# Two transformer blocks on one core: modulation steps placed one by one, more first products ahead, and the end of the first MLP loop rearranged

## The chip, the cores and the metric

The kernel runs on one core of a Trainium2 chip, as one program from inputs in device memory to the output in device memory. The metric is the device time of one execution in microseconds (us). Five engines work side by side and each runs its own instructions in a fixed order: PE (matrix products), DVE (VectorE), ACT (ScalarE), POOL (GpSimd) and SP (here only a queue that starts transfers). An instruction that waits holds up everything behind it on its engine. Engines meet through semaphores; a transfer (DMA) is issued by the queue of an engine and then moves by itself.

## The reference, cut to what matters

Two blocks follow one another on x of 1024 tokens by 1024 columns, all in float32. The work touched by the change is the MLP of the first block, that of the second, and the modulation of the second.

```python
def first_block(x, ...):
    ...
    x = x + jnp.einsum("bsd,de->bse", merged, w_out[l])
    h = rmsnorm(x, g_mlp[l])
    hid = jnp.square(jax.nn.relu(jnp.einsum("bsd,df->bsf", h, w_mlp_in[l])))     # 1024 x 1024 x 4096
    x = x + jnp.einsum("bsf,fd->bsd", hid, w_mlp_out[l])                         # 1024 x 4096 x 1024
    return rmsnorm(x, g_final)

def second_block(x, c, ...):
    mod = jax.nn.silu(c) @ w_ada[l] + b_ada[l]       # one row of 1024 times 1024 x 6144
    sh1, sc1, gt1, sh2, sc2, gt2 = jnp.split(mod, 6, axis=-1)
    h = _modulate(_rmsnorm(x, g_mix[l]), sh1, sc1)
    x = x + gt1[:, None, :] * _mixer(h, ...)
    h = _modulate(_rmsnorm(x, g_ffn[l]), sh2, sc2)
    a = jnp.square(jax.nn.relu(jnp.einsum('bsd,df->bsf', h, w_ff1[l])))
    x = x + gt2[:, None, :] * jnp.einsum('bsf,fd->bsd', a, w_ff2[l])
    return _rmsnorm(x, g_final)
```

## The kernel before, in words

In the time of the profiled execution the kernel has these stretches: attention of the first block up to about 700 us, the merge and the output projection to 880, the MLP of the first block (MLP1) to about 1640, the mixer of the second block to 2037, and the MLP of the second block (MLP2) to 2713. Both MLPs are the one function `mlp`, called twice.

The activations are held transposed (features on the 128 partitions, tokens along the row), and all matrices are split in two fp32r parts: hi is a cast, lo is what is left. A product is then three passes of the matrix engine, hi·hi, lo·hi and hi·lo. `product` (L1231 ff.) makes one 128 x 512 block over four feature chunks, so 4 x 3 = 12 matmuls of 128 x 512 (L1233 to L1235). `parts_of` splits a weight tile: the cast "wh" on ACT (L1227) and the rest "wl" on DVE, or on POOL where it is told so (L1228).

Each GEMM is done by a scheme of seven products for eight. In the first GEMM, 16 steps m run in a loop. The seven products of a step are P1 and P2 (both in `first_two`: P1 is copied to s1, P2 plus s1 becomes q11, L1264 to L1277), P5, and products with the operands t2, B22, t3 and t4. P1 and P2 need only the first half of the activations, HT[0]; the others need HT[1], t2, t3 and t4, all made from the second half. Those operands are made by `make_t` and, for its second part, `rest` (L1104 ff.), a chain of about 45 DVE instructions that begins when the row statistics of the second half have gone through POOL (L127) and a transpose on PE (L1035). `rest` holds four of the six product banks in PSUM for its intermediates. Before the loop, `first_two` is called for m = 0 to 3; from m = 3 on the loop calls it for m + 1. `sums` (L1279, its four additions at L1284 to L1287) makes the combined weight tiles on POOL. The results of a step, q11, q12, q21, q22, t1 to t4 and so on, are stored in device memory by `save` (L1258), on ACT's queue, with t1 to t4 put off to the next step by `later`.

In the second GEMM, four blocks `ch` of hidden columns run over seven products for each of four output tiles e. `second` (L1358 ff.) loads one stored operand of 1 MB and splits it: the cast at L1370, the difference at L1371, alternately on DVE and POOL. Weights w2 come in quarters of 1 MB by SP's queue (L1407), and the sums of quarters s_, a21 and a11 are made on POOL (L1432, L1450, L1451, L1454). The results of the products are added by DVE: `upd` (L1377) into the residual, which lies in the tiles that the loop used before, and is loaded from "ml_x" by 16 transfers (L1356); `gather` (L1388); L1460.

The modulation (`ada`, L1182 to L1209) is a row times a matrix, done on DVE: 12 groups of 8 steps. A step multiplies a 128 x 512 weight tile "adaw" (256 KB, loaded by SP's queue) by one number per partition and adds it to "ada" (L1199 the first, L1201 the others). After 8 steps PE transposes the group in four blocks (L1207), and DVE reduces and adds the bias (L1208, L1209). `tick` advances this generator by one step; the loop of MLP1 ticks four times per m, in two pairs.

Within an engine the instructions stand in an order that a scheduler of the builder has fixed from a model of durations; in program order the ticks are where the code calls them, but the scheduler moves an instruction whose inputs are there early. `order` rows, shown with the change, are that fixed order.

## Time and profile before

| | |
|---|---|
| median of 3 runs | 2725.16 us (2717.71 to 2726.5) |
| the profiled execution | 2721.95 us |
| its span in the trace | 2720.2 us |
| mean granted clock of PE | 0.972 of full speed |
| busy in the span: PE, DVE, ACT, POOL | 93%, 69%, 44%, 36% |

The profiled execution is 1.75 us longer than its span. Times in the views are microseconds from the start of the span. A clock of 1.00 is the upper level of PE's clock, 2.4 GHz; 0.50 would be the lower, 1.2 GHz, and a stretch with a value between has had both. A row on a wait says which engine and line waited for which other engine and line. Matmuls are pipelined, so the duration of one is longer than the spacing of two.

### The profile page before, as it was taken

To read this page: it belongs to the slowest core of one execution; us is meant where nothing else is said; L and a number is where in the kernel's file an instruction comes from. 1 tells how busy PE (TensorE), PEld (TensorE's weight loads), DVE (VectorE), ACT (ScalarE), POOL (GpSimd) and SP (SyncE) were. 2 spreads that over 40 slices of the span, in tenths; PEclk is the share of its full clock that TensorE was granted. 3 is DMA by queue.
4 is the path that set the end of the run, shared out by engine and by line. 5 is a ranking of instruction groups with operands and counts; after the bars stand their busy time and mean duration, and the time that the engine had idled before them with its cause. 6 is when DMAs were issued, how large, how long until landed. Compare 5 with 4: busy or idle time off the path is not lost. (4 is left out here: it accounts for less than half of the span.)

```text
span 2720.2 us, 34915 instructions
## 1 busy us (share of the span) xinstructions
PE 2528.9 (93%) x12560; PEld 2107.4 (77%) x12560; DVE 1882.7 (69%) x3206; ACT 1197.9 (44%) x2218; POOL 988.1 (36%) x717
## 2 busy tenths in 40 slices
PE   7999999899999678888899979999997999989997
PEld 6899987788878566667688856888786788768886
DVE  7685878834455866676778896755658565578898
ACT  6575765335334433334433333323335554543433
POOL 3011123421002533333755661211334443476554
PEclk9999999999999889999999989999998999999999
DMA  3121022321155266666644301422343444753431
GB/s 114 53 61 40 25 79 90 89 61 41 63 183 179 78 203 200 202 204 230 220 170 155 109 24 51 156 63 70 120 152 97 160 150 159 250 204 134 170 109 62
DMA packets 275712, 338.57 MB, mean 124 GB/s; under 512 B 14268, under 2 KB 185044, under 8 KB 268372
## 3 DMA queue, kind: packets, MB, share of 16 engines
q1 hardware_dynamic: 234820, 253.65, 29.2%
q10 hardware_dynamic: 40720, 82.70, 8.3%
q8 instruction: 99, 1.62, 0.2%
q14 instruction: 73, 0.60, 0.1%
HBM read 250.25 MB, written 86.05 MB: 124 GB/s over the span
## 5 line engine op out<-in xcount | busy, mean ns | idle before, releaser
L1233 PE MATMUL mm<-h_hi,wh 128*128 128x512 f32 (+1 forms) x1136 | 455.5, 401 | 33.3 <-ACT wh L1227 17.2
L1235 PE MATMUL mm<-h_hi,wl 128*128 128x512 f32 (+1 forms) x1136 | 452.1, 398 | 10.5 <-DVE wl L1228 10.5
L1234 PE MATMUL mm<-h_lo,wh 128*128 128x512 f32 (+1 forms) x816 | 322.2, 395 | 0.0
L1233 PEld LDWEIGHTS mm<-h_hi,wh 128*128 128x128 f32 x1136 | 221.4, 195 | 82.2 <-ACT wh L1227 20.6
L1235 PEld LDWEIGHTS mm<-h_hi,wl 128*128 128x128 f32 x1136 | 220.7, 194 | 63.4 <-DVE wl L1228 18.2
L1227 ACT CAST wh<-q 128x1024 fp32r<-128x1024 f32 x116 | 121.7, 1052 | 331.7 <-PE mm L1234 297.7
L1234 PE MATMUL mm<-h_hi,wh 128*128 128x512 f32 (+1 forms) x624 | 244.8, 392 | 13.2 <-POOL h_hi L1371 13.2
L1228 DVE TENSOR_TENSOR wl<-q,wh 128x1024 fp32r<-128x1024 f32 x116 | 162.9, 1405 | 32.9 <-ACT wh L1227 31.3
L1234 PEld LDWEIGHTS mm<-h_lo,wh 128*128 128x128 f32 x816 | 158.3, 194 | 31.6
L1371 POOL TENSOR_TENSOR h_hi<-h_lo,h_hi 128x512 fp32r<-128x512 f32 x76 | 128.6, 1712 | 113.1 <-ACT h_hi L1370 107.9
L133 ACT CAST wh<-wr 128x1024 fp32r<-128x1024 f32 (+5 forms) x107 | 97.2, 911 | 149.7 <-PE mm L418 43.5
L1233 PE MATMUL mm<-q,wh 128*128 128x512 f32 x384 | 151.3, 394 | 10.4 <-DVE q L1119 10.4
L1235 PE MATMUL mm<-q,wl 128*128 128x512 f32 x384 | 150.2, 392 | 8.0 <-DVE wl L1228 8.0
L1234 PE MATMUL mm<-q,wh 128*128 128x512 f32 x384 | 150.9, 393 | 0.0
L1234 PEld LDWEIGHTS mm<-h_hi,wh 128*128 128x128 f32 x624 | 120.5, 193 | 37.9 <-POOL h_hi L1371 14.4
L1284 POOL TENSOR_TENSOR sa<-wr 128x512 f32<-128x512 f32 x32 | 41.7, 1303 | 264.8 <-DMA wr<-in_w_ff_dram 60.5
L134 POOL TENSOR_TENSOR wl<-wr,wh 128x1024 fp32r<-128x1024 f32 (+5 forms) x40 | 78.1, 1958 | 160.7 <-ACT wh L133 159.2
L1615 PE MATMUL mm<-h_hi,wh 128*128 128x512 f32 x320 | 132.0, 412 | 0.8 <-DVE kn L1648 0.8
L1617 PE MATMUL mm<-h_hi,wl 128*128 128x512 f32 x320 | 126.7, 396 | 0.0
L1371 DVE TENSOR_TENSOR h_hi<-h_lo,h_hi 128x512 fp32r<-128x512 f32 x76 | 120.4, 1605 | 8.3 <-ACT h_hi L1370 8.3
L1616 PE MATMUL mm<-h_lo,wh 128*128 128x512 f32 x320 | 125.5, 392 | 0.0
L1233 PE MATMUL mm<-h_lo,wh 128*128 128x512 f32 (+1 forms) x304 | 115.4, 380 | 0.6 <-ACT wh L1227 0.6
(589 smaller groups left out, 7006.9 us busy)
## 6 DMA issues: line engine op xcount, KB each, us to landing
h_lo<-ml_t SPq DMA_DIRECT2D x32, 1024.0 KB
adaw<-in_w_ada_dram SPq DMA_DIRECT2D x96, 256.0 KB
h_lo<-ml_q SPq DMA_DIRECT2D x24, 1024.0 KB
wr<-in_w_in_dram SPq DMA_DIRECT2D x42, 512.0 KB
wr<-in_w_out_dram SPq DMA_DIRECT2D x32, 512.0 KB
ml_t<-h_lo ACTq DMA_DIRECT2D x64, 256.0 KB
q<-in_w_mlp_out_dram SPq DMA_DIRECT2D x16, 1024.0 KB
ml_t<-x ACTq DMA_DIRECT2D x64, 256.0 KB
```

Source lines behind the costliest of these rows:

```text
L133: A.copy(hi, r)
L134: (eng or V).tensor_tensor(lo, r, raw(hi), op=OP.subtract)
L1227: A.copy(hi, r)
L1228: (eng or V).tensor_tensor(lo, r, raw(hi), op=OP.subtract)
L1233: mm(a, wt[0][:, k], b[0][:, k, sl], start=(k == 0), stop=False)
L1234: mm(a, wt[0][:, k], b[1][:, k, sl], start=False, stop=False)
L1235: mm(a, wt[1][:, k], b[0][:, k, sl], start=False, stop=(k == 3))
L1284: G.tensor_tensor(sa[:, 0:4], e2[:, 0:4], e2[:, 4:8], op=OP.add)
L1371: (G if c % 2 else V).tensor_tensor(lo[:, c], r[:, c], raw(hi[:, c]), op=OP.subtract)
L1615: mm(a, hi[:, k, :], r_hi, start=(k == 0), stop=False)
L1616: mm(a, hi[:, k, :], r_lo, start=False, stop=False)
L1617: mm(a, lo[:, k, :], r_hi, start=False, stop=(k == DC - 1))
```

## The change

Four things are changed, and line numbers of the kernel after are larger by some 20 (matmuls L1255 to L1257, wh L1249, wl L1250).

1. The modulation steps (now L1180 and L1182). `tick` takes the result of an eviction, and the step is queued on DVE behind that eviction (`tc.issue_after`), one step at a time: four per m in MLP1's loop, the rest, 40 of 96 steps, in the first three blocks of the second GEMM. The tiles are loaded two steps ahead. The transpose of the bias and the silu of c move from the begin of MLP1 into the output projection.
2. `first_two` runs for m = 4, 5 and 6 first, with s1 and q11 stored in device memory ("away", ACT's queue), and then for 0 to 3: 14 products ahead of the first P5, in place of 8. The loop then loads s1 and q11 of 4, 5, 6 back by SP's queue in steps 3, 4 and 5.
3. The last step's put-off stores and those of q22 and q21, six in all, are issued on POOL's queue.
4. The residual comes back in four transfers of 1 MB, in place of 16 of 256 KB: `x_back(0)` behind the load of t1, `x_back(1)` behind that of t2; the additions of block 0 into the second half of the residual, `upd(1, e)`, move from the q12 products to the t2 products.

```diff
+        load(0)
+        load(1)
+        for g in range(12):
+            acc = modp([P, 512], tag="ada", bufs=1)
+            for k in range(DC):
+                w = ld.pop(0)
...
+                load(g * DC + k + 2)
+                yield
...
+    def tick1(after):
+        with tc.issue_after(after.ins):
+            next(ada_, None)
...
         def save(n, m, t_):
-            nc.scalar.dma_start(d[n][:, m, :], t_)
+            (nc.gpsimd if later and m == NM - 1 else nc.scalar).dma_start(d[n][:, m, :], t_)
...
+            if away:
+                nc.scalar.dma_start(d["away"][:, m - 4, 0, :], s1)
+                nc.scalar.dma_start(d["away"][:, m - 4, 1, :], q11)
...
-        first_two(0, w_of(wp, 0, "wr", 2))
+        first_of(4, away=True)
         begin[0]()
-        first_two(1, w_of(wp, 2, "wr", 2), begin[1])
-        first_two(2, w_of(wp, 4, "wr", 2), eng=G)
+        first_of(5, away=True)
+        begin[1]()
+        first_of(6, eng=G, away=True)
+        first_of(0)
         rest_t.pop()()
         begin[2]()
-        first_two(3, w_of(wp, 6, "wr", 2), eng=G)
+        first_of(1)
+        first_of(2)
+        first_of(3)
...
-                if m >= 3:
+                if m >= 6:
                     first_two(m + 1, e1s[m + 1])
+                elif m >= 3:
+                    for i, t_ in enumerate((s1s, q11s)):
+                        nc.sync.dma_start(t_[(m + 1) % 4], d["away"][:, m - 3, i, :])
...
-            V.tensor_tensor(q12, p5, u2, op=OP.add)
-            for _ in range(2):
-                tick()
+            tick(V.tensor_tensor(q12, p5, u2, op=OP.add))
             ub = parts_of(e1s.pop(m))
             a = mm_bank()
             product(a, half(ub, 1), B22)
-            V.tensor_tensor(q12, a, q12, op=OP.add)
+            tick(V.tensor_tensor(q12, a, q12, op=OP.add))
...
+        def x_back(hf):
+            for e0 in (0, 4):
+                nc.sync.dma_start(xt[hf][:, e0:e0 + 4, :], d["x"][:, e0:e0 + 4, halves(hf)])
...
             b = second("t2", ch)
+            if not ch:
+                x_back(1)
             for e, wt in blocks(a11):
                 a = mm_bank()
                 product(a, wt, b)
-                V.tensor_tensor(U[e], a, U[e], op=OP.add)
+                if not ch:
+                    upd(1, e, U[e])
+                r = V.tensor_tensor(U[e], a, U[e], op=OP.add)
+                if e != 1:
+                    tick(r)
```

First place: DVE at the head of MLP1, at the end of the chain of `rest`. The q_ names are t3 and t4; wl tiles with wr_ are weights of `first_two`, sa_ and we_ those of the loop. Before:

```order
L1119 TENSOR_TENSOR q_9108<-mm_9261,q_9107 128x512
L1143 TENSOR_TENSOR mm_9262<-t_1892_9189,mm_9262 128x512
L1274 TENSOR_TENSOR h_hi_8328<-mm_9340,h_hi_8328 128x512
L1228 TENSOR_TENSOR wl_9366<-sa_9360,wh_9365 128x1024
```

And now:

```order
L1120 TENSOR_TENSOR q_9118<-mm_9313,q_9117 128x512
L1144 TENSOR_TENSOR mm_9314<-t_1897_9219,mm_9314 128x512
L1295 TENSOR_TENSOR h_hi_8333<-mm_9392,h_hi_8333 128x512
L1250 TENSOR_TENSOR wl_9411<-wr_9408,wh_9410 128x1024
L1120 TENSOR_TENSOR q_9118<-mm_9314,q_9117 128x512
L1250 TENSOR_TENSOR wl_9447<-wr_9444,wh_9446 128x1024
L1295 TENSOR_TENSOR h_hi_8333<-mm_9428,h_hi_8333 128x512
```

Behind the chain there now stand wl_9411 and wl_9447, the weights of `first_of(2)` and `first_of(3)`, four products that are meant to run ahead of the loop. Before, no wl of `first_two` stood behind it: those of m = 0 and 1 came earlier on DVE, and those of 2 and 3 were made by POOL.

Second place: DVE in the loop, one step m. Before:

```order
L1209 TENSOR_TENSOR mod_9086<-mod_9086,bada_9087 128x4
L1228 TENSOR_TENSOR wl_9978<-we_9762,wh_9977 128x1024
L1201 SCALAR_TENSOR_TENSOR ada_10357<-adaw_10455,silu_9404,ada_10357 128x512
L1339 TENSOR_TENSOR h_lo_8329<-mm_9895,h_hi_8328 128x512
L1340 TENSOR_TENSOR h_lo_8329<-mm_9895,h_lo_8329 128x512
L1201 SCALAR_TENSOR_TENSOR ada_10357<-adaw_10458,silu_9404,ada_10357 128x512
L1201 SCALAR_TENSOR_TENSOR ada_10357<-adaw_10512,silu_9404,ada_10357 128x512
L1201 SCALAR_TENSOR_TENSOR ada_10357<-adaw_10515,silu_9404,ada_10357 128x512
L1201 SCALAR_TENSOR_TENSOR ada_10357<-adaw_10612,silu_9404,ada_10357 128x512
L1274 TENSOR_TENSOR h_hi_8328<-mm_9939,h_hi_8328 128x512
L1228 TENSOR_TENSOR wl_10000<-wr_9849,wh_9999 128x512
```

And now:

```order
L1345 TENSOR_TENSOR h_lo_8334<-mm_9617,h_hi_8333 128x512
L1182 SCALAR_TENSOR_TENSOR ada_9527<-adaw_9583,silu_8844,ada_9527 128x512
L1250 TENSOR_TENSOR wl_9737<-sa_9685,wh_9736 128x1024
L1349 TENSOR_TENSOR h_lo_8334<-mm_9658,h_lo_8334 128x512
L1182 SCALAR_TENSOR_TENSOR ada_9527<-adaw_9603,silu_8844,ada_9527 128x512
L1359 TENSOR_TENSOR h_lo_8334<-mm_9690,h_hi_8333 128x512
L1360 TENSOR_TENSOR h_lo_8334<-mm_9617,h_lo_8334 128x512
L1182 SCALAR_TENSOR_TENSOR ada_9527<-adaw_9652,silu_8844,ada_9527 128x512
L1250 TENSOR_TENSOR wl_9775<-we_9630,wh_9774 128x1024
L1365 TENSOR_TENSOR h_lo_8334<-mm_9711,h_lo_8334 128x512
L1182 SCALAR_TENSOR_TENSOR ada_9527<-adaw_9673,silu_8844,ada_9527 128x512
```

Four or more steps in a row, each waiting for its own tile, have become single steps with an eviction ahead of each.

Third place: POOL between the two GEMMs of MLP1. h_hi_ and h_lo_ with L1371 (now L1401) are operands of the second GEMM, q_ at L1432 to L1451 (now L1462 to L1484) the sums of weight quarters. Before:

```order
L1371 TENSOR_TENSOR h_hi_11911<-h_lo_11811,h_hi_11911 128x512
L1320 TENSOR_TENSOR h_lo_8329<-h_hi_8328,h_lo_8329 128x512
L1343 TENSOR_TENSOR h_lo_8329<-h_lo_8329 128x512
L1432 TENSOR_TENSOR q_11818<-q_11814,q_11816 128x1024 x2
L1450 TENSOR_TENSOR q_11814<-q_11812,q_11814 128x1024 x2
L1451 TENSOR_TENSOR q_11812<-q_11818,q_11812 128x1024 x2
L1371 TENSOR_TENSOR h_hi_11911<-h_lo_11811,h_hi_11911 128x512
```

And now:

```order
L1401 TENSOR_TENSOR h_hi_11836<-h_lo_11815,h_hi_11836 128x512
L1280 DMA ml_q_1745_8348<-h_lo_8334 128x512
L1401 TENSOR_TENSOR h_lo_11997<-h_lo_11815,h_lo_11997 128x512
L1280 DMA ml_q_1743_8346<-h_lo_8334 128x512
L1280 DMA ml_t_1744_8347<-h_lo_8334 128x512
L1373 TENSOR_TENSOR h_lo_8334<-h_lo_8334 128x512
L1280 DMA ml_t_1742_8345<-h_lo_8334 128x512
L1280 DMA ml_t_1746_8349<-h_lo_8334 128x512
L1462 TENSOR_TENSOR q_11822<-q_11818,q_11820 128x1024 x2
L1483 TENSOR_TENSOR q_11818<-q_11816,q_11818 128x1024 x2
L1484 TENSOR_TENSOR q_11816<-q_11822,q_11816 128x1024 x2
```

The second half of the operand h_hi (before: h_hi_11911, now: h_hi_11836) has moved from behind the six sums to ahead of them, and DMA issues stand between.

## Rows read from the trace of the kernel before

**Rows 1.** The profile's head and its busy times by engine.

```profile
span 2720.2 us, 34915 instructions
PE 2528.9 (93%) x12560; PEld 2107.4 (77%) x12560; DVE 1882.7 (69%) x3206; ACT 1197.9 (44%) x2218; POOL 988.1 (36%) x717
```

**Rows 2.** The view by stretches: stretch, its length, busy time (count) of PE, of PE's weight loads, of DVE, ACT and POOL, granted clock, share of DMA, GB/s. In order: head and loop of MLP1, the passage to its second GEMM, a part of that GEMM, and, inside it, a part with nothing but full-speed products; then head, loop and passage of MLP2.

```profile
880.00:983.00 103.00, 67.22 (x268) 52.96 (x267) 81.31 (x102) 39.70 (x64) 48.16 (x32) 0.82 0.41 133
983.00:1293.00 310.00, 272.08 (x1136) 214.59 (x1134) 213.55 (x278) 124.94 (x188) 110.74 (x78) 0.96 0.62 206
1293.00:1345.00 52.00, 42.93 (x167) 33.82 (x168) 36.70 (x38) 21.94 (x34) 38.53 (x18) 0.88 0.73 260
1360.00:1564.00 204.00, 204.00 (x901) 168.92 (x901) 172.70 (x174) 80.12 (x115) 121.73 (x61) 1.00 0.41 145
1428.00:1496.00 68.00, 68.00 (x301) 56.31 (x301) 59.88 (x59) 27.17 (x40) 39.42 (x20) 1.00 0.43 155
2037.70:2121.00 83.30, 64.08 (x261) 50.34 (x260) 61.23 (x79) 43.32 (x70) 42.45 (x30) 0.88 0.33 100
2121.00:2370.70 249.70, 247.92 (x1093) 204.72 (x1092) 141.53 (x174) 129.67 (x189) 108.80 (x79) 1.00 0.53 176
2370.70:2423.40 52.70, 42.91 (x168) 33.76 (x169) 37.47 (x38) 21.99 (x35) 38.72 (x18) 0.90 0.73 264
```

**Rows 3.** PE's waits at the head of MLP1 (880 to 983 us): engine, line that waited, what it waited for, us in total, times, longest.

```profile
PE tp L1207 <- DVE ada L1201: 13.8, 2, 12.2
PE tp L1035 <- POOL st_r L127: 10.2, 1, 10.2
PE mm L1233 <- ACT h_hi L1269: 6.1, 1, 6.1
PE mm L1233 <- DVE q L1119: 5.7, 1, 5.7
```

**Rows 4.** The same view in the loop of MLP1 (983 to 1293 us).

```profile
PE mm L1235 <- DVE wl L1228: 14.2, 16, 1.9
PE tp L1207 <- DVE ada L1201: 12.6, 7, 2.1
PE mm L1233 <- ACT wh L1227: 10.9, 4, 6.0
```

**Rows 5.** DVE's longest wait in that loop, same columns.

```profile
DVE ada L1201 <- DMA adaw<-in_w_ada_dram: 57.0, 32, 4.1
```

**Rows 6.** DVE's groups of instructions in that loop: line, operation, output and inputs, shape, count, busy time and mean duration in ns, then the idle time before them.

```profile
L1201 DVE SCALAR_TENSOR_TENSOR ada<-adaw,silu,ada 128x512 f32<-128x512 f32 x70 | 55.5, 793 | 57.6 <-DMA adaw<-in_w_ada_dram 57.0
L1209 DVE TENSOR_TENSOR mod<-mod,bada 128x4 f32<-128x4 f32 x11 | 12.7, 1155 | 0.0
L1208 DVE TENSOR_REDUCE mod<-tp 128x4 f32<-128x512 f32 x11 | 7.4, 676 | 0.0
```

**Rows 7.** DVE's groups in the second GEMM (1360 to 1564 us), same columns.

```profile
L1228 DVE TENSOR_TENSOR wl<-q,wh 128x1024 fp32r<-128x1024 f32 x38 | 51.0, 1341 | 3.7 <-ACT wh L1227 3.6
L1371 DVE TENSOR_TENSOR h_hi<-h_lo,h_hi 128x512 fp32r<-128x512 f32 x26 | 42.6, 1664 | 0.0
L1377 DVE TENSOR_TENSOR h_lo<-mm,h_lo 128x512 f32<-128x512 f32 x36 | 24.2, 681 | 15.6 <-PE mm L1235 15.6
```

**Rows 8.** The timeline of DVE at the head of MLP1: start, us, line, operation, output and inputs, count. The first row is the first instruction behind the transpose L1035, the second the last of the chain of `rest`; the others are a wl and modulation steps right behind it.

```profile
900.19 1.41 DVE L1109 SCALAR_TENSOR_TENSOR h_lo<-h_lo,cols,tp 128x512 f32<-128x512 f32 x2 [6.83 <-PE tp L1035]
...
931.61 0.68 DVE L1119 TENSOR_TENSOR q<-mm,q 128x512 fp32r<-128x512 f32 x1
...
934.11 1.78 DVE L1228 TENSOR_TENSOR wl<-wr,wh 128x512 fp32r<-128x512 f32 x1
935.81 3.47 DVE L1201 SCALAR_TENSOR_TENSOR ada<-adaw,silu,ada 128x512 f32<-128x512 f32 x2
```

**Rows 9.** The timeline of POOL at the head of MLP1, up to the statistics (L127).

```profile
889.11 1.71 POOL L1284 TENSOR_TENSOR sa<-wr 128x512 f32<-128x512 f32 x1
...
897.96 1.02 POOL L127 TENSOR_TENSOR st_r<-st_r,mhalf 128x4 f32<-128x4 f32 x1
```

**Rows 10.** PE's waits between the GEMMs of MLP1 (1293 to 1345 us).

```profile
PE mm L1234 <- POOL h_hi L1371: 7.4, 1, 7.4
PE mm L1233 <- ACT wh L1227: 6.0, 1, 6.0
```

**Rows 11.** The timeline of POOL there.

```profile
1300.43 5.20 POOL L1432 TENSOR_TENSOR q<-q,q 128x1024 f32<-128x1024 f32 x2 [0.40 <-DMA q<-in_w_mlp_out_dram]
...
1311.29 6.07 POOL L1451 TENSOR_TENSOR q<-q,q 128x1024 f32<-128x1024 f32 x2
1317.32 1.26 POOL L1371 TENSOR_TENSOR h_hi<-h_lo,h_hi 128x512 fp32r<-128x512 f32 x1
```

**Rows 12.** The timeline of ACT there: the cast of the first weight quarter, what it waited for, and a store's issue by ACT's queue.

```profile
1275.33 0.33 ACTq L1258 DMA_DIRECT2D ml_t<-h_lo  x1
...
1291.90 1.04 ACT L1227 CAST wh<-q 128x1024 fp32r<-128x1024 f32 x1 [7.49 <-DMA q<-in_w_mlp_out_dram]
```

**Rows 13.** The waits of SP's queue from 1262 to 1320 us (the loads of the residual, L1356).

```profile
SPq L1356 <- DVE h_lo L1339: 10.1, 2, 8.8
```

**Rows 14.** PE's waits at the head of MLP2 (2037.7 to 2121 us).

```profile
PE mm L1233 <- ACT x L1269: 8.2, 1, 8.2
PE mm L1233 <- DVE q L1119: 4.7, 1, 4.7
```

**Rows 15.** PE's waits between the GEMMs of MLP2 (2370.7 to 2423.4 us).

```profile
PE mm L1234 <- POOL h_hi L1371: 5.8, 1, 5.8
PE mm L1233 <- ACT wh L1227: 3.6, 2, 1.8
```

More of the change, by code (lines that the diff above doesn't have):

```diff
@@ L1145, in make_t, with ada, load @@
         rest_t.append(rest)
+    mod = cst([P, 48], tag="mod")
+    bada = cst([P, 48], tag="bada")
+    def ada(modp):
+        badr = modp([48, P], tag="badr")
+        nc.scalar.dma_start(badr, b_ada_2[0].rearrange("(k p) -> k p", p=P))
+        yield
+        pt = tp_bank()
+        T.transpose(pt[:, :48], badr, ident[:48, :48])
+        V.tensor_copy(bada, pt[:, :48])
+        r0, _ = ROWS["c_2"]
+        s_ = modp([P, 64], tag="silu")[:, :DC]
+        A.activation(s_, cols[:, r0:r0 + 8], AF.Tanh, scale=0.5)
+        V.scalar_tensor_tensor(s_, s_, 1.0, cols[:, r0:r0 + 8], op0=OP.add, op1=OP.mult)
+        V.tensor_scalar(s_, s_, 0.5, None, op0=OP.mult)
+        yield
+        ld = []
+        def load(i):
+            if i < 12 * DC:
+                w = modp([P, 512], tag="adaw", bufs=2)
+                nc.sync.dma_start(w, w_ada_2[0, (i % DC) * P:(i % DC + 1) * P, halves(i // DC)])
+                ld.append(w)
+        load(0)
[4 more added lines that the diff above has]
+                w = ld.pop(0)
+                if k == 0:
+                    V.tensor_scalar(acc, w, s_[:, 0:1], None, op0=OP.mult)
+                else:
+                    V.scalar_tensor_tensor(acc, w, s_[:, k:k + 1], acc, op0=OP.mult, op1=OP.add)
+                load(g * DC + k + 2)
+                yield
+            yield
+            m4 = mod[:, g * 4:(g + 1) * 4]
+            pt = tp_bank()
+            for j in range(4):
+                T.transpose(pt[:, j * P:(j + 1) * P], acc[:, j * P:(j + 1) * P], ident)
+            V.tensor_reduce(m4, pt.rearrange("p (j q) -> p j q", j=4), axis=AX.X, op=OP.add)
+            V.tensor_tensor(m4, m4, bada[:, g * 4:(g + 1) * 4], op=OP.add)
+    modp = Pool("modp", side="right")
+    ada_ = ada(modp)
+    def tick1(after):
+        with tc.issue_after(after.ins):
+            next(ada_, None)
     xT = [hB([P, DC, 512], tag=n) for n in ("h_hi", "h_lo")]
@@ L1162, in x_cols @@
         A.copy(xT[hf][:, e, :], pt)
+        if e == 2:
+            next(ada_)
     mlp_d = mlp_dram(drm)
@@ L1257, in save, with first_two @@
         def save(n, m, t_):
[L1258 removed]
+            (nc.gpsimd if later and m == NM - 1 else nc.scalar).dma_start(d[n][:, m, :], t_)
         def save_later():
             while later:
[L1262 to L1264 removed]
+                save(*later[0])
+                later.pop(0)
+        def first_two(m, e1, eng=None, away=False):
             s1, q11 = s1s[m % 4], q11s[m % 4]
@@ L1327, in mlp @@
             V.tensor_tensor(u3, a, u2, op=OP.add)
-            V.tensor_tensor(q22, p5, u3, op=OP.add)
+            tick(V.tensor_tensor(q22, p5, u3, op=OP.add))
             relu2(q22)
             save("q22", m, q22)
-            for _ in range(2):
-                tick()
             a = mm_bank()
             product(a, u4, TQ["t4"])
-            V.tensor_tensor(u3, a, u3, op=OP.add)
+            tick(V.tensor_tensor(u3, a, u3, op=OP.add))
             A.activation(u3, u3, AF.Relu)
@@ L1433, in mlp @@
             b = second("q12", ch)
+            if not ch:
+                bt = second("t1", ch)
+                x_back(0)
             for e, wt in blocks(a11):
@@ L1534, in post_mlp1 @@
         if hf == 0:
-            for _ in ada_["it"]:
+            for _ in ada_:
                 pass
```

75 lines of the change are left out of this document (16 added, 59 removed).

## The prediction

> **What bounds the kernel now.** I read the busy times first: PE is busy for 2528.9 of the 2720.2 us, DVE for 69% [rows 1]. So time can only come from PE's gaps and from the time in which PE runs below its full clock. For where these lie I read the view by stretches. Between 1428 and 1496 us PE does 301 matmuls of 128 x 512 in 68.00 us at a clock of 1.00: 0.226 us each, 2.71 us for a product of 12 [rows 2]. What a stretch loses is its length less its matmuls times 0.226, and this counts gaps and slow clock together:
> - head of MLP1: 103.0 - 268 x 0.226 = 42 us, clock 0.82;
> - loop of MLP1: 310.0 - 1136 x 0.226 = 53 us, clock 0.96;
> - passage to its second GEMM: 52.0 - 167 x 0.226 = 14 us, clock 0.88;
> - the second GEMM, 1360 to 1564: nothing, 901 x 0.226 = 204;
> - head of MLP2: 83.3 - 261 x 0.226 = 24 us; its loop: 249.7 - 1093 x 0.226 = 3 us; its passage: 52.7 - 168 x 0.226 = 15 us [all rows 2].
>
> Together 151 us, of which the change touches all. The two loops are the same code, and only that of MLP1 has modulation steps: 53 us against 3. Last I read, for each of these stretches, which wait of PE it is (rows named below).
>
> **The change part by part.**
>
> *Modulation in the loop.* PE waits 14.2 us in 16 pieces for wl, 12.6 us for the last step of a group and 10.9 us for wh, 37.7 us together [rows 4]; the other 15 of the 53 are the slower clock behind each gap. The first two come from DVE's order: steps stand four or more in a row, and each can wait for its tile. DVE stood 57.0 us in 32 such waits, 1.8 us each, the longest 4.1 [rows 5]; behind the waiting step stand the wl and the evictions that PE needs. Afterwards one step stands behind each of four evictions per m, and its tile was asked for two steps earlier. DVE's load allows it: in MLP2's loop it works 141.5 of 249.7 us [rows 2], about 10.8 us in the 19.0 of a step m; four modulation steps of 0.793 and half a group's end of (0.676 + 1.155) [rows 6] add 4.1. What stays: two of the seven group ends in this loop have their transposes directly behind the product of the eviction before the last step, and wh is untouched by this part. I put the loop at 12 us (from 53), between 5 (a little over MLP2's 3) and 25 (both wh and group ends as before: 10.9 + 12.6): -41.
>
> *More P1 and P2 ahead.* At the head PE waits 13.8 us for modulation steps, 10.2 for the statistics on POOL, 6.1 for an ACT result of `first_two` and 5.7 for the chain of `rest` [rows 3]. The first goes: no transpose of a group stands there now. Of the second, POOL's sums, 889.1 to 897.9 us before L127 [rows 9], go behind it, some 8 us, and what is late next is the reduce on DVE. The third is hidden by more products. But the cover for the chain is thinner than 14 products. The chain takes from 900.2 to 932.3 us, 32 us, of DVE with hardly a gap [rows 8]. Behind the transpose L1035 PE has six products, 6 x 2.71 = 16 us; the weights of the next four, wl_9411 and wl_9447, stand behind the chain in DVE's order. So PE stands for about 32 - 16 = 16 us, where the slower clock then adds 3 to 4. Head from 42 to 20 us, -22. Bounds: 12 if only the chain's first part is waited for, 28 if the loop's wl, which follow those two, come late too. In MLP2 the same order holds; its 24 us, 8.2 of them for ACT and 4.7 for the chain [rows 14], become 20: -4, between -10 and +2.
>
> The stores and loads of s1 and q11 for 4 to 6 are 12 more transfers of 256 KB. They lie beside the head and the loop, where the DMA engines have shares of 0.41 and 0.62 [rows 2]; I cost them at nothing. Without that cover, 1.5 MB each way at the loop's 206 GB/s is 15 us.
>
> *The passage.* In MLP1 PE waits 7.4 us for the second half of an operand that POOL makes only behind six sums of weights, from 1300.4 to 1317.3 us, and 6.0 us for the first weight quarter's cast [rows 10, 11]. That cast stood 7.5 us for its transfer [rows 12], since SP's queue was held by the residual's loads, which waited 10.1 us for tiles still in use [rows 13]. Now the operand is ahead of the sums and the loads behind the quarters, so both waits go. What is late next: the wl of a11 stands in DVE's order ahead of the evictions of the t1 products, and needs the same sums. They start behind six DMA issues, which this trace shows nowhere on POOL. Bounds for one: 0.33 us, what an issue takes on ACT's queue [rows 12], and 3.04, half of the two L1451 in 6.07 [rows 11], the longest POOL instruction here. 2 to 18 us in all; I take the lower, since the row is a DMA issue as well. `x_back(1)` waits for these stores, and DVE's additions into the second half wait for it; before them PE has about eight products, 22 us. The passage goes from 14 to 9. In MLP2 (15 us, of which 5.8 and 3.6 [rows 15]) there is no modulation: to 10. Together -10.
>
> The Trainium skill has a rule against these stores (the page "SBUF — State Buffer", the box on the trap "DVE blocks DMA", and "DMA: Bandwidth & Descriptors", section "Anatomy of one DMA — SWDGE (gpsimd) path"): a DMA from POOL's queue has its descriptors made by POOL itself in software, at about 2.0 us fixed, and DVE can keep it from that. No row here shows such a DMA; by 2.0 us the six would be 12 us, and the total about 10 us higher.
>
> *Modulation in the second GEMM.* Here the change costs. 40 steps and five group ends go into blocks 0 to 2, some 65 products or 65 x 2.71 = 176 us. DVE works there 172.7 of 204 us [rows 2], 149 in 176. 40 steps of 0.8 are 32 us and five ends of 1.83 are 9: 190, over the 176. And the steps may be longer than in the loop, because POOL works 121.7 of 204 us here (60%) against 110.7 of 310 (36%) [rows 2]: the wl of 1024 columns takes 1341 ns, the difference L1371 of 512 columns 1664 with POOL doing its twin, an eviction 681 [rows 7]. Bounds for a step: 0.79 [rows 6] and 1.74, the two of 3.47 at the head [rows 8]. I take 1.0, near the wl, whose length per column is what a step is like: 149 + 40 + 9 = 198, 22 too many. The products ahead in the banks and split tiles absorb some 6 to 9 us; 13 to 16 come through as gaps, with the slower clock (53 / 37.7 = 1.4 in the loop) 18 to 22. +19, between 0 (DVE's waits give way) and +60 (1.74: 149 + 70 + 9 = 228, 52 too many).
>
> On this the same page of the Trainium skill, section "SBUF: two separate sides", says that a DVE instruction with two inputs in SBUF and a POOL instruction that reads SBUF exclude each other, and the later one waits for the whole of the other. The rows agree where they can: L1371, two inputs in SBUF, takes 1664 ns, and an eviction, with one in PSUM, 681 [rows 7]. By it each of the 35 steps with two tiles waits for a rest of POOL's work as L1371 does, 35 x (1.66 - 1.0) = 23 us more on DVE, and with the slower clock the total comes to about 2693.
>
> *The sum.* -41 - 22 - 4 - 10 + 19 = -58. Against the profiled execution, 2721.95 us (span 2720.2 and 1.75 around it), that is 2664; the median of the runs shown, 2725.2, is 3 higher, so the same step from there is 2667. I forecast 2664.
>
> **The rivals.**
> *The second GEMM takes the steps for nothing, and the cover at the head holds.* For it: DVE's idle time there is mostly waiting for PE (15.6 us for one line [rows 7]), and the scheduler may have put the steps there. Against it: 190 us of work in 176. Then the loop ends at 5, the head at 12, MLP2's head at 16, the passages at 5 and 8, nothing on top: 53 + 42 + 24 + 29 - 46 = 102 less, 2620.
> *POOL's queue is dear.* Each issue at 3.04 instead of 0.33 holds the sums, the stores and the residual 16 us longer, and with the clock PE loses 22 to 25: 2688. Against it: the stores are few.
> *Little changes.* The waits move with the steps: the loop keeps half (27 us), the second GEMM loses 45, the head falls only to 28 since the chain alone is 32 us: -26 + 45 - 14 = +5 and so 2727. For it: DVE has as many instructions as before.
> *Slower.* One mechanism: the 40 steps in the second GEMM each take 1.74 us [rows 8] and wait 1.8 for their tile (57.0 / 32 [rows 5]), because the loads stand in SP's queue between loads that wait for tiles. That is 40 x 3.5 + 9 = 149 us on a DVE with 176 - 149 = 27 free: 122 over, which outweighs all gains (77) and ends at 2765. It decides from about 2.3 us a step on (40 x 2.3 + 9 - 27 = 74). Against it: loads two ahead, and a share of DMA of 0.41 there.
>
> **How the numbers follow.** The forecast 0.55, its own range 2638 to 2692; the first rival 0.16; POOL's queue 0.12; little change 0.08; slower 0.09. The range for 8 in 10 leaves out the slower rival and the lower edge of the first: 2615 to 2708. A measurement of this kernel tells about 0.3%, 8 us, from no change. Faster than that: 0.55 + 0.16 + 0.12 + 0.02 = 0.85; the same 0.05; slower 0.10.
>
> **What would show it.** Loop of MLP1: a clock of 0.99 or more, PE's wait for modulation under 4 us, DVE's wait for adaw under 10. Head: one wait of 12 to 18 us behind the six products, for wl or the chain. Passage: no wait for L1401 on POOL, and sums L1462 that start right behind the stores. Second GEMM: DVE busy over 95% in the blocks with steps, PE waiting for wl and for DVE's differences in small pieces, clock below 1.00. Wrong would make it: steps of 1.5 us or more there, POOL idle for tens of us at the stores, or DVE standing for the residual.

## The result and the profile after

The changed kernel takes 2683.84 us (median of 4 runs, 2677.26 to 2685.34) beside 2725.26 us for the kernel before: a ratio of 0.9849, with a 95% interval of 0.9825 to 0.9873, so 41 us or 1.5% faster. The forecast was 2664 us, with a range of 2615 to 2708. The profiled execution has a span of 2683.1 us, 37.1 less than before.

The head of the page of the kernel after, for [rows 1]; the second line is the new queue, by its page's third part:

```profile
span 2683.1 us, 34924 instructions
PE 2522.5 (94%) x12560; PEld 2108.3 (79%) x12560; DVE 1905.7 (71%) x3208; ACT 1198.5 (45%) x2218; POOL 985.1 (37%) x727
...
q0 software_dynamic: 960, 3.15, 0.3%
```

The view by stretches of the kernel after, for [rows 2]. The cuts lie at the same numbers of products as there: an MLP has 224, of which the head has the first 21, the loop 91, the passage 14 and the stretch behind it, of the second GEMM, 91 again. The lines are head, loop, passage and second GEMM of MLP1, then head and loop together, and the passage, of MLP2.

```profile
880.00:955.70 75.70, 63.11 (x262) 50.57 (x261) 53.60 (x73) 38.00 (x61) 30.96 (x22) 0.89 0.34 104
955.70:1237.90 282.20, 258.54 (x1122) 211.17 (x1120) 212.29 (x254) 129.17 (x192) 126.94 (x87) 0.97 0.67 217
1237.90:1297.90 60.00, 46.50 (x172) 36.52 (x173) 48.94 (x50) 20.77 (x32) 35.98 (x22) 0.83 0.73 272
1297.90:1556.30 258.40, 251.95 (x1110) 207.52 (x1109) 239.42 (x244) 95.22 (x138) 160.20 (x78) 0.99 0.46 160
2000.50:2336.30 335.80, 317.06 (x1354) 258.24 (x1353) 198.55 (x255) 173.27 (x260) 146.95 (x108) 0.96 0.50 166
2336.30:2386.60 50.30, 42.95 (x169) 34.17 (x168) 46.36 (x34) 21.08 (x33) 37.25 (x24) 0.90 0.70 259
```

The same 91 products of MLP1's second GEMM in the kernel before, which no row ahead of the prediction has:

```profile
1345.30:1592.80 247.50, 247.50 (x1093) 204.95 (x1092) 211.35 (x203) 95.08 (x138) 158.21 (x79) 1.00 0.36 128
```

Length against length, in us: MLP1's head 103 to 75.7 (27 less), its loop 310 to 282.2 (28 less), its passage 52 to 60.0 (8 more), its second GEMM 247.5 to 258.4 (11 more); MLP2's head and loop 83.3 + 249.7 = 333.0 to 335.8 (3 more), its passage 52.7 to 50.3 (2 less). That is 35 of the 37 us: 57 gained, 22 given back.

PE's waits in the kernel after: the head of MLP1, its loop, its passage, its second GEMM and MLP2's passage, for [rows 3, 4, 10, 15].

```profile
PE mm L1255 <- ACT h_hi L1292: 6.3, 1, 6.3
PE mm L1255 <- DVE q L1120: 5.7, 1, 5.7
...
PE tp L1189 <- DVE ada L1182: 15.8, 3, 8.8
PE mm L1255 <- ACT wh L1249: 4.9, 3, 3.8
PE mm L1257 <- DVE wl L1250: 2.9, 2, 2.4
...
PE mm L1257 <- DVE wl L1250: 9.7, 1, 9.7
PE mm L1255 <- ACT wh L1249: 3.8, 1, 3.8
PE tp L1189 <- DVE ada L1182: 3.6, 1, 3.6
...
PE tp L1189 <- DVE ada L1182: 6.1, 3, 3.5
...
PE mm L1257 <- DVE wl L1250: 7.4, 3, 4.9
```

The 16 small waits for wl in the loop are two now, and PE's waits for POOL are gone from both passages. In their place stands one wait of 9.7 us for wl. DVE's timeline has this wl beside POOL's sums in the kernel before:

```profile
1306.74 2.33 DVE L1228 TENSOR_TENSOR wl<-q,wh 128x1024 fp32r<-128x1024 f32 x1 [3.37 <-ACT wh L1227]
```

and in the kernel after, with POOL's timeline behind it:

```profile
1252.28 10.41 DVE L1250 TENSOR_TENSOR wl<-q,wh 128x1024 fp32r<-128x1024 f32 x1 [8.61 <-ACT wh L1249]
```

```profile
1243.52 0.54 POOL L1280 DMA_DIRECT2D ml_t<-h_lo  x1
1244.07 1.31 POOL L1373 TENSOR_TENSOR h_lo<-h_lo 128x512 f32<-128x512 f32 x1
1245.31 1.09 POOL L1280 DMA_DIRECT2D ml_t<-h_lo  x2
1246.42 4.74 POOL L1462 TENSOR_TENSOR q<-q,q 128x1024 f32<-128x1024 f32 x2
1251.11 4.68 POOL L1483 TENSOR_TENSOR q<-q,q 128x1024 f32<-128x1024 f32 x2
1255.75 4.62 POOL L1484 TENSOR_TENSOR q<-q,q 128x1024 f32<-128x1024 f32 x2
1260.34 1.26 POOL L1401 TENSOR_TENSOR h_lo<-h_lo,h_lo 128x512 fp32r<-128x512 f32 x1
```

One wl of 1024 columns, 1.2 us of work, lasts 10.41 us: it begins while POOL runs its sums and ends 1.1 us after POOL has come to rest at 1261.6. POOL's sums are not slowed, 2.3 us each, where [rows 11] have 2.6 and 3.0 for one. Before, DVE got in between two sums (2.33 us for the wl); here it did not until POOL paused. In MLP2's passage the like wl lasted 13.5 us. The rest of this text calls this the lock-out.

### The profile page after: what moved, and what is told of

It is laid out like the page before. It is cut to its first block, busy times and chain, and to the rows that moved or that the text cites. A ratio compares the mean times of both kernels' runs of the same rounds, so it can differ in the third digit from the quotient of the medians.

```text
span 2683.1 us, 34924 instructions
## 1 busy us (share of the span) xinstructions
PE 2522.5 (94%) x12560; PEld 2108.3 (79%) x12560; DVE 1905.7 (71%) x3208; ACT 1198.5 (45%) x2218; POOL 985.1 (37%) x727
## 5 line engine op out<-in xcount | busy, mean ns | idle before, releaser
L1255 PE MATMUL mm<-h_hi,wh 128*128 128x512 f32 (+1 forms) x1136 | 456.3, 402 | 33.6 <-DVE q L1120 10.3
L1257 PE MATMUL mm<-h_hi,wl 128*128 128x512 f32 (+1 forms) x1136 | 452.0, 399 | 22.8 <-DVE wl L1250 22.8
L1255 PEld LDWEIGHTS mm<-h_hi,wh 128*128 128x128 f32 x1136 | 221.9, 195 | 82.8 <-ACT wh L1249 13.0
L1257 PEld LDWEIGHTS mm<-h_hi,wl 128*128 128x128 f32 x1136 | 221.4, 195 | 75.3 <-DVE wl L1250 29.6
L1249 ACT CAST wh<-q 128x1024 fp32r<-128x1024 f32 x116 | 122.0, 1053 | 345.3 <-PE mm L1256 294.3
L1250 DVE TENSOR_TENSOR wl<-q,wh 128x1024 fp32r<-128x1024 f32 x116 | 192.2, 1659 | 22.4 <-ACT wh L1249 21.0
L1401 POOL TENSOR_TENSOR h_hi<-h_lo,h_hi 128x512 fp32r<-128x512 f32 x76 | 126.2, 1679 | 127.8 <-ACT h_hi L1400 127.6
L1255 PE MATMUL mm<-q,wh 128*128 128x512 f32 x384 | 150.1, 391 | 0.0
L1257 PE MATMUL mm<-q,wl 128*128 128x512 f32 x384 | 149.6, 390 | 0.0
L1250 DVE TENSOR_TENSOR wl<-we,wh 128x1024 fp32r<-128x1024 f32 x50 | 79.1, 1582 | 59.8 <-ACT wh L1249 55.9
L1255 PE MATMUL mm<-h_lo,wh 128*128 128x512 f32 (+1 forms) x304 | 115.4, 380 | 0.6 <-ACT wh L1249 0.6
L598 ACT ACTIVATE sbit<-sbit 128x1024 bf16<-128x1024 bf16 (+2 forms) x99 | 93.6, 947 | 50.0 <-DVE sbit L597 48.1
```

The source lines that it names most:

```text
L598: A.activation(b, b, AF.Copy, accum_out=cnt[:, j:j + 1])
L1249: A.copy(hi, r)
L1250: (eng or V).tensor_tensor(lo, r, raw(hi), op=OP.subtract)
L1255: mm(a, wt[0][:, k], b[0][:, k, sl], start=(k == 0), stop=False)
L1257: mm(a, wt[1][:, k], b[0][:, k, sl], start=False, stop=(k == 3))
L1401: (G if c % 2 else V).tensor_tensor(lo[:, c], r[:, c], raw(hi[:, c]), op=OP.subtract)
```

## The experiments

Each kernel is compared with the kernel before on the same chip, by the ratio to it; the changed kernel has 0.9849 (0.9825 to 0.9873). Differences to the changed kernel are by the medians unless it says by the ratios. Where no interval is told, the kernel was run once. Lengths of stretches that no line shows are from the same view, cut at the same products.

**The stores on ACT's queue again.**

```diff
-            (nc.gpsimd if later and m == NM - 1 else nc.scalar).dma_start(d[n][:, m, :], t_)
+            nc.scalar.dma_start(d[n][:, m, :], t_)
```

> The changed kernel with one part undone: the last step's stores go through ACT's queue again, so POOL has no DMA. Theory A: the DMAs on POOL's queue keep DVE away from POOL's stretch of sums behind them; in the changed kernel one wl there lasts 10.4 us in MLP1 and one 13.5 us in MLP2. Then here no wl there is longer than about 3.4 us, PE's waits for wl of 9.7 and 4.9 us go, and with the clock behind them the time falls by 12 to 22 us. Theory B: the stretch of sums without a gap between them does it, whoever issues the stores; then a wl of 9 us or more stays, since the sums stand as close here, and the time stays within 5 us. Theory C: stores on ACT delay its casts, and the time rises by up to 10 us.

Measured: ratio 0.9853 (0.9836 to 0.9869), as the changed kernel. DVE's timeline, with the two wl that stand at this place:

```profile
1249.14 5.63 DVE L1250 TENSOR_TENSOR wl<-q,wh 128x1024 fp32r<-128x1024 f32 x2 [10.28 <-ACT wh L1249]
```

No wl is over 3.5 us, so theory A holds for the mechanism, and its time fails. PE's waits in this passage:

```profile
PE mm L1257 <- DVE wl L1250: 8.1, 4, 3.7
PE tp L1189 <- DVE ada L1182: 4.5, 1, 4.5
PE mm L1255 <- ACT wh L1249: 4.1, 2, 3.9
```

One wait of 9.7 us has become four of 8.1 together: DVE and POOL now take turns, each 512 or 1024 columns wide, and DVE falls behind in pieces. The lengths of the two passages, MLP1's and MLP2's, where the changed kernel has 60.0 and 50.3:

```profile
1234.50:1294.30 59.80, 46.78 (x172) 36.41 (x173) 45.74 (x47) 20.16 (x32) 36.47 (x17) 0.84 0.75 273
2338.20:2385.20 47.00, 42.20 (x167) 33.01 (x168) 37.81 (x32) 20.68 (x32) 34.24 (x16) 0.93 0.69 257
```

So without the lock-out MLP1's passage is as long as with it. MLP2's is 3 us shorter, and the loop before it takes 2 of them back.

**The stores on POOL's queue alone, on the kernel before.** The edit is the same line of `save`, and in `save_later` a store leaves the list only after it is issued, as in the changed kernel.

> The kernel before with the stores of the last step on POOL's queue and nothing else. If a DMA on POOL's queue is what keeps DVE out of the sums behind it, a wl of 9 us or more shows in both passages, where the kernel before has none over 2.4 us. The builder's order puts the second half of the operand ahead of the sums here as well, so PE's wait of 7.4 us for POOL goes and one for wl of 7 to 10 comes: within 8 us of the kernel before. If the kernel before's other order protects it, no wl is over 3.5 us and the time falls by 8 to 15 us.

Measured: ratio 1.0036 (1.0023 to 1.005), 10 us slower. DVE's timeline and PE's waits in MLP1's passage:

```profile
1307.46 10.41 DVE L1228 TENSOR_TENSOR wl<-q,wh 128x1024 fp32r<-128x1024 f32 x1 [7.53 <-ACT wh L1227]
```

```profile
PE mm L1235 <- DVE wl L1228: 9.7, 1, 9.7
PE mm L1233 <- ACT wh L1227: 7.8, 2, 6.2
```

The wait for POOL's operand (7.4 us, [rows 10]) is gone and 9.7 us for wl have come, as the first theory said, with the time just over its 8 us. In all, eight of the kernels run, the changed one among them, issue the six stores on POOL, and each has a wl of 10.4 to 13.5 us in both passages; five issue them on ACT or SP, the kernel before among them, and none has one over 3.5 there. That a DMA on POOL's queue brings the lock-out is shown; by what means it outlasts the issue, which in MLP1 ended 6 us before the wl began, is not.

**One store on POOL's queue.** On a kernel with 8 products ahead and late folds (both below), only t4's store is POOL's.

> 8 products ahead, folds late, five of the six stores on ACT's queue and only t4's on POOL's, which stands between the sums. If one DMA of POOL's is enough to lock DVE out until POOL next stands still, the first DVE instruction with two inputs in SBUF behind it lasts until the end of the sums: 5 us or more in both passages. If it takes several, or their data's movement, nothing is over 3.5 us.

Measured: 2657.18 us in one run. In MLP1's passage DVE was in the middle of a wl when the DMA was issued, and took turns with POOL, at most 3.1 us a wl. In MLP2's the timelines of DVE and POOL show:

```profile
2330.59 7.05 DVE L1253 TENSOR_TENSOR wl<-q,wh 128x1024 fp32r<-128x1024 f32 x1 [5.95 <-ACT wh L1252]
```

```profile
2324.04 0.65 POOL L1283 DMA_DIRECT2D ml_t<-x  x1
2324.72 4.76 POOL L1481 TENSOR_TENSOR q<-q,q 128x1024 f32<-128x1024 f32 x2
2329.43 2.54 POOL L1398 TENSOR_TENSOR h_lo<-h_lo,h_lo 128x512 fp32r<-128x512 f32 x2
2331.93 4.62 POOL L1484 TENSOR_TENSOR q<-q,q 128x1024 f32<-128x1024 f32 x2
```

So one DMA was enough in MLP2, where DVE came 6 us behind it into an unbroken run of POOL's, and not in MLP1, where DVE was already at work beside POOL. The expectation had both passages alike; each of its halves came true in one. With two places in one run, it stays open which difference between them decides.

**The transposes that fold a modulation group, later.**

```diff
             yield
+            yield
             m4 = mod[:, g * 4:(g + 1) * 4]
             pt = tp_bank()
-            for j in range(4):
-                T.transpose(pt[:, j * P:(j + 1) * P], acc[:, j * P:(j + 1) * P], ident)
+            with tc.issue_after(last_mm[0].ins):
+                for j in range(4):
+                    T.transpose(pt[:, j * P:(j + 1) * P], acc[:, j * P:(j + 1) * P], ident)
...
-                mm(a, wt[1][:, k], b[0][:, k, sl], start=False, stop=(k == 3))
+                last_mm[0] = mm(a, wt[1][:, k], b[0][:, k, sl], start=False, stop=(k == 3))
```

> The changed kernel with the four transposes that end a modulation group put one step later and queued on PE behind the product that was last in the program there. Theory A: PE stands at these transposes for nothing else than the last step on DVE (8.8, 3.5, 3.6, 3.6, 1.2, 1.4 and 3.5 us in the changed kernel); then all seven waits go and with the slower clock behind them the time falls by 25 to 35 us. Theory B: the operands of the product behind the transposes are as late (the wl behind the 8.8 us one was ready only 1.8 us before the transposes ran), and DVE as a whole is behind; then the waits move to wl and wh, and the time falls by 3 to 12 us.

Measured: ratio 0.9794 (0.9779 to 0.9808), 2667.05 us, 17 less than the changed kernel. PE's waits in its loop and then in its second GEMM:

```profile
PE mm L1258 <- ACT wh L1252: 7.6, 5, 2.8
PE mm L1260 <- DVE wl L1253: 5.5, 6, 2.4
...
PE mm L1260 <- DVE wl L1253: 2.5, 2, 1.4
```

Of the seven waits of transposes, 25.5 us with the passage's, six went and the one in the passage fell from 3.6 to 1.2. Some 7 us of them came back as waits for wh and wl in the loop (13.1 against 7.8) and in the second GEMM (2.5), and 3 as waits for wl in the passage (12.7 against 9.7). It lies between the two theories: PE did stand for a transpose that nobody needed yet, and a part of that time it would have waited anyway, but not most of the 8.8 us that theory B saw: no wait in the loop is over 2.8. The added `yield` also moves modulation steps: the loop has 47 in place of 53, the second GEMM 38 in place of 30, and still both stretches are shorter (272.2 and 253.1 us, from 282.2 and 258.4).

**8 products ahead in place of 14.**

```diff
-        first_of(4, away=True)
+        first_of(0)
         begin[0]()
-        first_of(5, away=True)
+        first_of(1)
         begin[1]()
-        first_of(6, eng=G, away=True)
-        first_of(0)
+        first_of(2, eng=G)
         rest_t.pop()()
         begin[2]()
-        first_of(1)
-        first_of(2)
-        first_of(3)
+        first_of(3, eng=G)
...
-                if m >= 6:
+                if m >= 3:
```

(and without the loads back in steps 3 to 5).

> The changed kernel with 8 products ahead of the first P5, as before the change, in the order 0, 1, 2, 3, and no storing and loading of s1 and q11. The prediction's step on the heads says that the six more products are worth the larger part of 22 + 4 us: then this is 15 to 30 us slower than the changed kernel. If the gain at the head comes from the modulation's leaving it (13.8 us of PE's waits before), this is within 8 us of the changed kernel.

Measured: ratio 0.9802 (0.9787 to 0.9816), 2669.70 us: 14 us faster than the changed kernel, where 15 to 30 slower was one theory and 8 either way the other. Both fall. The view by stretches for products 21 to 49 of MLP1 and then of MLP2, with 14 ahead (the changed kernel) and with 8:

```profile
955.70:1054.50 98.80, 82.54 (x345) 66.35 (x344) 71.45 (x88) 39.34 (x58) 46.17 (x31) 0.93 0.72 233
2075.40:2164.70 89.30, 82.60 (x337) 65.76 (x336) 47.42 (x64) 40.11 (x58) 39.61 (x31) 0.94 0.60 199
```

```profile
967.10:1043.80 76.70, 76.70 (x342) 63.49 (x341) 60.89 (x72) 38.47 (x56) 33.42 (x24) 1.00 0.63 198
2071.40:2149.50 78.10, 76.78 (x338) 62.94 (x337) 45.83 (x57) 39.67 (x58) 34.83 (x25) 1.00 0.52 172
```

With 8 ahead, PE runs these 28 products at full speed; with 14 it takes 22 and 11 us more. The heads go the other way, 90.2 and 81.2 us with 8 ahead against 75.7 and 74.9 with 14: 21 us gained, 33 lost. (In MLP1, 8.8 of the 22 is the transposes' wait, which with 8 ahead lies in the head, as 8.3.) The six products were not added, they were taken out of the steps m = 3, 4 and 5. A step then has five products, 13.6 us of PE, beside the rest of its evictions, weight tiles, sums and stores, where seven products had 19.0. That the loss lies in this stretch and goes with this part is shown. Whether the short steps' other work or the loads back of s1 and q11 make it, no run tells apart; in MLP2's stretch the profile has no wait of any engine that ended with a transfer, which speaks for the steps' other work.

**The wl of m = 2 and 3 on POOL.**

```diff
-        first_of(2)
-        first_of(3)
+        first_of(2, eng=G)
+        first_of(3, eng=G)
```

> The changed kernel with the wl of P1 and P2 for m = 2 and 3 made on POOL, so that they do not stand behind the chain of differences on DVE. If PE's two waits at the head (6.3 and 5.7 us in MLP1, 6.8 and 4.6 in MLP2) come from these two wl, PE has ten products in place of six beside the chain, and both waits go: 10 to 18 us off each head, 20 to 36 us together. If they come from the chain itself and from its use of four PSUM banks, the products wait for banks instead, and the time changes by less than 6 us.

Measured: ratio 0.9864 (0.985 to 0.9879), 2 us slower than the changed kernel, with intervals that overlap. PE's wait at the head of MLP1 in this run:

```profile
PE mm L1255 <- ACT h_hi L1292: 14.0, 2, 9.5
```

and the end of ACT's timeline in the changed kernel, with the instruction for which PE waits there:

```profile
913.46 0.66 ACT L1119 CAST h_hi<-h_lo 128x512 fp32r<-128x512 f32 x1
913.98 0.63 ACT L1292 COPY h_hi<-mm 128x512 f32<-128x512 f32 x1
```

The copy of P1 (L1292), which frees a product bank, stands on ACT behind the casts of the chain (L1119), and `rest` holds four of the six banks. The wl was not what PE waited for: with it out of the way, both waits are for the copy.

**Two more banks for P1.** With 14 ahead, late folds, and the wl of m = 2 and 3 on POOL, P1 of these two goes to the banks of the transposes.

```diff
-            a = mm_bank()
+            a = (tp_bank if spare else mm_bank)()
             product(a, half(u, 0), B11)
             A.copy(s1, a)
```

> 14 products ahead as in the changed kernel, folds late, the wl of m = 2 and 3 on POOL, and P1 of m = 2 and 3 in the two PSUM banks that the transposes use. If the heads wait for banks (rest holds four of six, and the copy that frees one stands on ACT behind the casts of the chain: 6.3 and 6.8 us, 9.5 and 8.4 with the wl on POOL), PE gets two to four products more beside the chain and this is 10 to 20 us faster than the run with late folds alone (2667.1). If the banks are no limit, within 4 us of it.

Measured: ratio 0.9774 (0.9758 to 0.9791) beside 0.9794 (0.9779 to 0.9808) for late folds alone: 5 us by the ratios, 7 by the medians, with intervals that overlap, and between the two theories. PE's waits at MLP1's head:

```profile
PE mm L1258 <- DVE q L1120: 7.4, 1, 7.4
PE mm L1258 <- ACT h_hi L1295: 3.1, 1, 3.1
```

The waits for the copy, 14.0 us in wl_on_pool, fell to 3.1, and PE came all the sooner to the wait for the chain's last operands. Both heads are shorter than with late folds alone, 72.2 and 70.3 us against 75.5 and 74.9. So banks are one limit of the head; that the 32 us of the chain [rows 8] are the next is read from the waits, and no run tests it. What this is worth in the whole time is not clear of the noise.

**The residual in 16 pieces again**, ahead of the second GEMM, and block 0's additions with the q12 products.

> The changed kernel with the residual loaded in 16 pieces at the loop's end again and block 0's additions with the q12 products. The prediction's step says that SP's queue, held by these loads, delays the first weight quarter: then PE waits 5 to 8 us for wh in the passage again, in each MLP, and the time rises by 6 to 14 us. If the starved wl hides it, the time stays within 5 us.

Measured: ratio 0.9894 (0.9879 to 0.9909) against 0.9849, 12 us slower by the ratios. PE waits for wh 9.4 us in MLP1's passage in place of 3.8:

```profile
PE mm L1257 <- DVE wl L1250: 9.7, 1, 9.7
PE mm L1255 <- ACT wh L1249: 9.4, 2, 6.6
```

That the wait comes back is as the prediction's step on SP's queue had it. Where the time goes is less plain: MLP2's passage is 5 us longer than in the changed kernel (55.3 against 50.3) and the last 63 products of each loop 3 us, but MLP1's passage is 4 us shorter (55.6 against 60.0), with no wait at a transpose in it. In MLP1's passage, then, the part costs time.

**The modulation's order alone, on the kernel before.**

> The kernel before with the first part of the change alone: modulation steps one by one behind evictions, tiles two ahead, the rest in the second GEMM, the begin in the output projection; 8 products ahead, stores on ACT's queue, residual in 16 transfers. Theory A (the modulation's order is the whole gain): 2665 to 2680, as fast as the run with 8 products ahead that has the two other parts too (2669.7). Theory B (the stores on POOL and the residual in four pieces give half of it): 2690 to 2705.

Measured: ratio 0.9827 (0.9809 to 0.9845), 2673.01 us, 47 less than before. Theory A: this part by itself brings as much as the whole change; that it brings more is not clear of the intervals. The view by stretches for MLP1's loop, and all of PE's waits there:

```profile
969.10:1231.10 262.00, 252.69 (x1117) 208.24 (x1115) 199.04 (x236) 127.16 (x188) 111.59 (x78) 0.99 0.65 211
```

```profile
PE tp L1189 <- DVE ada L1182: 3.5, 1, 3.5
```

By the ratios the change then adds up from 47 us for the order, some 7 for the stores and the residual together (0.9802 of the kernel with 8 ahead against 0.9827), and 13 lost by 14 products ahead: 41.

**Both helpful edits together: 8 ahead and late folds.**

> The changed kernel with both edits that helped: 8 products ahead, and the folding transposes later. If their gains (14 and 17 us) add, 2653 or so. If both remove the same waits in the steps m = 3 to 5, where steps without the two first products have 13.6 us of PE work for one m's modulation and evictions, then 2658 to 2668.

Measured: ratio 0.9754 (0.9734 to 0.9774), 2654.11 us. The gains add.

**The same with the last stores on ACT's queue, and on SP's.**

> 8 products ahead, folds late, and the last step's stores on ACT's queue. No wl over 3.5 us in the passages. If what the starved wl costs (9.7 and 6.5 us of PE's waits) is only changed into waits for ACT, as it was in the run with stores on ACT, 2650 to 2658, as with the stores on POOL (2654.1); if with less modulation in the way it comes through, 2635 to 2645.

> The same with these six stores on SP's queue, which has nothing else to issue there but loads that come later anyway. Then neither POOL's lock nor ACT's queue costs: no wl over 3.5 us, and 2635 to 2648. If SP, waiting for the last store's data, holds the loads of the weight quarters, PE waits for wh by 4 us or more in the passages and the time is 2655 to 2670.

Measured: 0.9753 (0.9738 to 0.9767) on ACT, 0.9741 (0.9722 to 0.976) on SP, beside 0.9754 on POOL. On ACT the time is that of the first half of its expectation, though in MLP1's passage PE then waits mostly for wl (6.5 us) and transposes (3.4), and less for ACT (2.7). On SP no wl is over 3.5 us and no wait for wh is over 1.4 in either passage, yet the 2650.56 us lie between the two figures expected, and the three intervals do not tell the three queues apart. All three are faster than the kernel before by 2.5% and than the changed one by 1.0%.

The lengths of the stretches where the queue and the residual's part show, in us:

| kernel | queue of the last stores | transfers of the residual | passage of MLP1 | passage of MLP2 | MLP1's second GEMM | last 63 products of MLP2's loop |
|---|---|---|---|---|---|---|
| before | ACT | 16 | 52.3 | 52.7 | 247.5 | 173.3 |
| before (pool_stores_alone) | POOL | 16 | 54.4 | 55.7 | 247.5 | 174.2 |
| order_alone | ACT | 16 | 53.4 | 53.4 | 260.6 | 173.2 |
| changed (residual_16) | POOL | 16 | 55.6 | 55.3 | 258.9 | 174.4 |
| changed | POOL | 4 | 60.0 | 50.3 | 258.4 | 171.4 |
| changed (stores_act) | ACT | 4 | 59.8 | 47.0 | 260.0 | 173.5 |
| late folds | POOL | 4 | 59.4 | 50.3 | 253.1 | 171.4 |
| 8 ahead and late folds | POOL | 4 | 58.9 | 50.3 | 252.9 | 171.4 |
| 8 ahead and late folds | ACT | 4 | 55.2 | 47.2 | 256.6 | 173.5 |
| 8 ahead and late folds | SP | 4 | 54.6 | 47.9 | 255.6 | 171.4 |

In MLP1's passage late folds alone or the stores off POOL alone take away 1 us at most, both together 4 or 5. PE's waits there are 17.1 us in the changed kernel, 16.7 with the stores on ACT, 16.2 with late folds, and 12.6 (ACT) and 11.8 (SP) with both: what one edit takes away comes back as another wait. And what the passages gain without the lock-out, the second GEMM and, on ACT, MLP2's loop mostly take back.

## Why the prediction was right, and where its steps were not

The time lay in the range, 20 us above the forecast. By the spans the gain is 37 us where the sum said 58. Term by term:

- *Modulation in the loop*, forecast 41 us: 28. That the order of the steps was the loss is shown (order_alone), and there the step holds in size too: the loop takes 262.0 us, 10 us stay where the forecast let 12 stay (262.0 - 1117 x 0.226), the clock is 0.99, and PE's only wait is one of 3.5 us at a transpose. In the changed kernel DVE's waits for its tiles, 57.0 us [rows 5], are 2.6, and PE's waits for wl 14.2 to 2.9 [rows 4], but 29 us stay (282.2 - 1122 x 0.226). What failed is how the parts meet: the step did not see that steps 3 to 5, robbed of two products each, have less PE work to hide behind; the term for part 2 counted only what the six products cover at the head. The waits at group ends, of which the step had named two without a price, are three and 15.8 us, with the slower clock behind them.
- *More P1 and P2 ahead*, forecast 22 + 4: the head of MLP1 gave 27, of which 12 came with the order alone (91.4 us in order_alone) and 8 are the transposes' wait that moved from the head into the loop. The stretch behind it took back more than the rest, and MLP2 lost 3. The part as a whole costs 14 us (eight_ahead). Six products behind L1035 and then a stall was right, and its size too (6.3 + 5.7 = 12.0 and the clock, for 16 + 3), in two waits where one was forecast. The step put the stall down to two wl behind the chain, and its signs named the chain as well. The wl were not it: wl_on_pool moved them and nothing was gained. The first wait is for a PSUM bank, freed by a copy behind ACT's casts; the second is for the chain's last operand.
- *The passage*, forecast 10 less: 8 more in MLP1, 2 less in MLP2. The waits for POOL's operand went as said. One step that failed is the price of the DMAs on POOL's queue: it asked what an issue takes on POOL (0.54 us measured, by the rows above; 0.33 was taken and 3.04 was the bound) and not what it does to DVE, which stood 9 and 12 us longer over one wl. But this is not the whole miss: by the table the stores on POOL's queue cost 2 and 3 us a passage on the kernel before, and in the changed kernel nothing in MLP1 and 3 us in MLP2. The other is the residual's part. It is worth 12 us by the ratios and 5 in MLP2's passage, as forecast; in MLP1's passage the wait for wh fell as said, and yet the passage is 4 us longer with it. There PE waits 3.6 us at a group's transposes that it does not wait for in order_alone and residual_16: 10 of the 40 modulation steps, which the prediction had put into the second GEMM, lie in this passage. The rest stays open. The rival on POOL's queue came nearest in time (2688), but that is luck: an issue took a sixth of its 3.04 us, the sums ran faster and not later, and it was DVE that stood.
- *Modulation in the second GEMM*, forecast 19 more: 11, with 30 of the 40 steps in it. A step took 1.29 us, not 1.0, between the bounds:

```profile
L1182 DVE SCALAR_TENSOR_TENSOR ada<-adaw,silu,ada 128x512 f32<-128x512 f32 x27 | 34.9, 1294 | 1.2 <-DMA adaw<-in_w_ada_dram 1.2
```

  Still PE waited almost only at transposes (6.1 us), not at wl or differences: DVE was busy 239.42 of 258.4 us (93%), where the sum had it 22 us over its time. The slower rival needed 2.3 us a step and waits for tiles; its tiles came (1.2 us of waiting).

That the time fell into the range owes something to luck as well. The loop, MLP2's head and the passages came out 13, 7 and 16 us dearer than their terms, MLP1's head and the second GEMM 5 and 8 cheaper, and the range is 93 us wide. In the slower rival the sum is 2 us off: 45 us more than 2721.95 are 2767, not 2765.

In the loop the same step took 1.04 us, against 0.79 before [rows 6]. On this the Trainium skill, page "SBUF — State Buffer", section "SBUF: two separate sides", bore out better than I weighed it: a DVE instruction with two inputs in SBUF and a POOL instruction that reads SBUF exclude each other for whole instructions. The steps agree (0.74 us alone in the timeline, most of those beside POOL 1.15 to 1.5, the longest 2.6). The lock-out of 10.4 us goes further than the rule, which has the later one wait for the other instruction: here the other was five instructions in a row. The box on the trap "DVE blocks DMA", on the same page of the Trainium skill, speaks of DVE keeping POOL from its descriptors; these runs show it the other way round, DVE standing behind a DMA of POOL's (10.41 us, pool_stores_alone). The 2.0 us that the prediction took from the Trainium skill, page "DMA: Bandwidth & Descriptors", section "Anatomy of one DMA — SWDGE (gpsimd) path", were misread: that section gives them for a whole transfer, most of it the wait for the last write, and not for POOL's time; here an issue took POOL 0.54 us.

## What to carry to other kernels

Work that is moved ahead to cover a stall is taken from a place where it covered something too; look at what the step it leaves still has to hide. A PE instruction that nobody needs soon, such as a transpose of a side computation, belongs behind as many products as there are, since PE's queue stops for it. A DMA on POOL's queue is priced by what POOL's next instructions do to DVE, not by its issue. And a long wait is not yet lost time: the lock-out came with 10 us on the kernel before, and undoing it gained nothing on the changed one, where other waits stood in the same place.
